# A streaming row sum: four rows per partition in the first load instead of one

## The chip, the cores and the metric

The kernel runs on one core of one Trainium2 chip. The metric is the device time of one execution in microseconds (us); the median of three runs stands for it. GB/s are 10^9 bytes per second, KiB and MiB are powers of two.

## The reference

```python
batch, seq, dim = 32, 512, 1024
x = np.random.randn(batch, seq, dim).astype(np.float32)
multiplier = 0.5

def reference(x, multiplier):
    return (np.sum(x, axis=-1) * multiplier).astype(np.float32)
```

So 16384 rows of 1024 float32 values (67.1 MB) are read, each is summed and multiplied by 0.5, and 64 KiB are written.

## The kernel before

The 16384 rows are spread over 128 partitions, 128 rows each. They are read in three groups, all on one DMA queue, issued by SyncE (SP):

- **The lead**: one row per partition, the last 128 rows of `x`, into a buffer of its own (`lead`). It is the first load (512 KiB, 4 KiB for each partition).
- **Seven blocks** (`b` = 0 to 6) of B = 16 rows per partition, 8 MiB each, 64 KiB for each partition. Partition p owns 112 consecutive rows of `x`, so a partition's piece of a block is contiguous. Blocks rotate through three buffers, `buf[b % 3]`. The load of block b from 3 on waits on SP until DVE (VectorE) has reduced block b - 3 (`freed`, line 122).
- **The tail**: the remaining 15 rows per partition (`tail = B - 1`), 15 consecutive rows of `x` for each partition. It is loaded in three pieces of 7, 5 and 2 rows into the buffer that block 4 has left (`pieces`, line 157), and the fifteenth row comes in two parts of 608 and 416 columns into `end` (line 162). All five loads are issued in a row once block 4 is reduced.

The sums are made as follows.

- The lead is summed on DVE before block 0 (line 128). The sums lie in column 0 of `lead_sq`, 32x32 transposes (line 129) turn them into 4 rows of 32 values, and these are stored as 4 pieces of 128 B.
- A block is one `reduce_sum` on DVE over 16 rows (line 134) and one small multiplication (line 140). In block 6, DVE takes 8 rows and ACT (ScalarE) the other 8, one `activation` with an accumulator for each row (`act_row`, line 90).
- The tail's rows are shared out by hand (`on_act`, line 175): DVE sums a row by adding its two halves with an accumulator (`dve_sum`, line 100), ACT with `act_row`. The end row is summed by DVE in two steps, `first` and `final`, where `final` also adds the result of `first`.

There are three stores, all on SP's queue: `early` for the 112 rows per partition of the blocks (line 167, after block 6), `lead_store` (line 171) right behind it, and `store` for the tail (line 195), after the last sum. SP then waits for all three to land, and the kernel ends.

Before the kernel is built, the loads that wait for nothing (the lead and blocks 0 to 2) are moved into the program's entry block, so that SP issues them ahead of the start barrier (`start_loads_at_entry`).

Of the kernel before, what the change touches and what calls it, by code (L numbers as in the profile page):

```python
# [9 lines left out]
def kernel(  # L10
# [13 lines left out]
    nc = tc.nc  # L24
# [4 lines left out]
    P = nc.NUM_PARTITIONS  # L29
# [3 lines left out]
    x_flat = x.flatten_outer_dims()  # L33
    N, D = x_flat.shape
    rows = N // P
    out_flat = out.rearrange("b s -> (b s)")
    mul = float(multiplier)

    B = 16
    n_blocks = rows // B  # L40
    assert N == P * rows and rows == n_blocks * B
    own = rows - B
    tail = B - 1
    lead0 = P * (own + tail)
    x_rows = x_flat[0 : P * own, :].rearrange("(p c) d -> p c d", p=P)
    x_last = x_flat[P * own : lead0, :].rearrange("(p c) d -> p c d", p=P)
    x_lead = x_flat[lead0:N, :]
    out_rows = out_flat[0 : P * own].rearrange("(p c) -> p c", p=P)
    out_last = out_flat[P * own : lead0].rearrange("(p c) -> p c", p=P)
    out_lead = out_flat[lead0:N].rearrange("(q c) -> q c", c=32)  # L50

    def sbuf(name, *shape):
        return ctx.enter_context(nc.sbuf_tensor(name, list(shape), fp32)).ap()

    bufs = 3
    buf = [sbuf(f"xb{i}", P, B, D) for i in range(bufs)]
    sums = sbuf("sums", P, rows)
    res = sbuf("res", P, rows)
    cut = 608
    at = 640  # L60
    end = sbuf("end", P, at + D - cut)
    S = 32
    lead = sbuf("lead", P, D)
    lead_sq = sbuf("lead_sq", P, S)
    lead_tr = sbuf("lead_tr", P, S)

    def sem(name):
        return nc.alloc_semaphore(name=name)

    dve_done = sem("dve_done")  # L70
    act_done = sem("act_done")
    counts = {"dve": 0, "act": 0}

    def marks(i, engine):

        s = dve_done if engine == "dve" else act_done
        i.then_inc(s, 1)
        counts[engine] += 1
        return counts[engine]

    def load(name, dst, src, free=None):
        landed = sem(name)
        i = nc.sync.dma_start(out=dst, in_=src)  # L83
        if free is not None:
            i.wait_op(dve_done, free, "sem-ge")
        i.then_inc(landed, 16)
        return landed

    def act_row(t, r, col):
        return nc.scalar.activation(  # L90
            out=t[:, r, :],
            in_=t[:, r, :],
            func=mybir.ActivationFunctionType.Copy,
            scale=mul,
            accum_out=res[:, col : col + 1],
        )

    def dve_sum(row, dst, scale):
        mid = row.shape[-1] // 2
        return nc.vector.tensor_tensor_reduce(  # L100
            out=row[:, 0:mid],
            in0=row[:, 0:mid],
            in1=row[:, mid:],
            scale=scale,
            scalar=0.0,
            op0=ADD,
            op1=ADD,
            accum_out=dst,
        )

    marks(nc.vector.memset(end[:, at - 2 : at], 0.0), "dve")  # L111
    zeroed = marks(nc.vector.memset(lead_sq, 0.0), "dve")  # L112
    freed = []
    lead_landed = load("lead_landed", lead, x_lead)
    for b in range(n_blocks - 1):
        c0 = b * B
        t = buf[b % bufs]
        landed = load(
            f"landed{b}",
            t,  # L120
            x_rows[:, c0 : c0 + B, :],
            freed[b - bufs] if b >= bufs else None,
        )
        h = B if b < n_blocks - 2 else B // 2
        if b == 0:
            nc.vector.wait_ge(lead_landed, 16)
            nc.vector.wait_ge(dve_done, zeroed)
            summed = marks(dve_sum(lead, lead_sq[:, 0:1], mul), "dve")
            turned = nc.vector.transpose(out=lead_tr, in_=lead_sq)  # L129
            turned.wait_op(dve_done, summed, "sem-ge")  # L130
            marks(turned, "dve")
        nc.vector.wait_ge(landed, 16)
        done = marks(
            nc.vector.reduce_sum(  # L134
                out=sums[:, c0 : c0 + h], in_=t[:, 0:h, :], axis=mybir.AxisListType.X
            ),
            "dve",
        )
        freed.append(done)
        scaled = nc.vector.tensor_single_scalar(  # L140
            out=res[:, c0 : c0 + h],
            in_=sums[:, c0 : c0 + h],
            scalar=mul,
            op=mybir.AluOpType.mult,
        )
        scaled.wait_op(dve_done, done, "sem-ge")
        early_dve = marks(scaled, "dve")
        if h < B:
            nc.scalar.wait_ge(landed, 16)
            for r in range(h, B):  # L150
                i = act_row(t, r, c0 + r)
            early_act = marks(i, "act")

    c0 = (n_blocks - 1) * B
    t = buf[(n_blocks - 1) % bufs]
    nc.sync.wait_ge(dve_done, freed[n_blocks - 1 - bufs])
    pieces = [(0, 7), (7, 12), (12, 14)]
    landed = [
        load(f"landed_p{k}", t[:, lo:hi, :], x_last[:, lo:hi, :])
        for k, (lo, hi) in enumerate(pieces)  # L160
    ]
# [6 lines left out]
    early.wait_op(act_done, early_act, "sem-ge")  # L168
    early_stored = sem("early_stored")
    early.then_inc(early_stored, 16)  # L170
    lead_store = nc.sync.dma_start(out=out_lead, in_=lead_tr[0:P:S, :])
    lead_stored = sem("lead_stored")
    lead_store.then_inc(lead_stored, 16)

    on_act = {4, 5, 6, 10, 11, 13}
    for k, (lo, hi) in enumerate(pieces):
        on = [r for r in range(lo, hi) if r in on_act]
        nc.scalar.wait_ge(landed[k], 16)
        for r in on:
            i = act_row(t, r, c0 + r)  # L180
        late_act = marks(i, "act") if k == len(pieces) - 1 else None
        on = [r for r in range(lo, hi) if r not in on_act]
        nc.vector.wait_ge(landed[k], 16)
        for r in on:
            dve_sum(t[:, r, :], res[:, c0 + r : c0 + r + 1], mul)
# [1 line left out]
    first = dve_sum(end[:, 0:cut], end[:, at - 1 : at], 1.0)  # L187

    first.then_inc(landed_end[1], 1)
    final = dve_sum(end[:, at - 2 :], res[:, rows - 2 : rows - 1], mul)  # L190
    final.wait_op(landed_end[1], 17, "sem-ge")
    done = marks(final, "dve")

# [71 lines left out]
```

## Time and profile before

| what | value |
|---|---|
| median of 3 runs | 160.72 us (160.58 to 160.73) |
| the profiled execution | 160.62 us |
| its span, first to last instruction | 159.3 us |
| DVE busy | 120.2 us (75%), 39 instructions |
| ACT busy | 16.3 us (10%), 29 instructions |
| DMA packets | 2168, 67.18 MB, mean 422 GB/s |
| time of the packets, share of 16 engines' span | 98.0% |

The profile shows one execution. The span leaves out what lies before the first and behind the last instruction, 1.3 us here. The busy time of an engine counts its instructions of arithmetic only; the DMA share is the mean busy share of the core's 16 DMA engines. The timeline gives the start of every instruction in us from the start of the span, and in brackets how long its engine had been idle and what ended that. A DMA issue has a time to landing, from the issue on SP to the semaphore that tells that all data is there.

### The profile page before, as it was taken

The page shows a single profiled execution, that of the slowest core. Times are in us where ns is not written, and L with a number is a line of the kernel's source. Part 1 is how long each engine was busy: PE and PEld are TensorE (multiplying, and loading weights), DVE is VectorE, ACT ScalarE, POOL GpSimd, SP SyncE. Part 2 cuts the span into 40 slices and gives each one's busy share as a digit, 9 for nine tenths or more (in the row PEclk, how much of TensorE's full clock was granted, in tenths as well). Part 3 has the DMA queues.
Part 4 walks back from the last instruction along what each step waited for, and adds up shares of the span by engine and source line. Part 5 has one row for each costly group of instructions (what it writes and reads, how often), then busy time and mean ns, then how long its engine had stood idle before and what let it go on. Part 6 is the DMA issues. An engine that isn't in the chain of part 4 may idle for free.

```text
span 159.3 us, 128 instructions
## 1 busy us (share of the span) xinstructions
DVE 120.2 (75%) x39; ACT 16.3 (10%) x29; POOL 0.2 (0%) x4
## 2 busy tenths in 40 slices
DVE  2000029999499995999869997899959999599744
ACT  2000000000000000000000000000000000099844
POOL 0000000000000000000000000000000000000000
DMA  9969989899699699699699898996996996999994
GB/s 395 510 280 527 411 379 527 379 411 527 263 527 527 263 527 527 263 527 494 296 527 428 362 527 379 411 527 280 510 527 263 527 527 263 436 403 433 442 397 144
DMA packets 2168, 67.18 MB, mean 422 GB/s; under 512 B 504, under 2 KB 632, under 8 KB 888
## 3 DMA queue, kind: packets, MB, share of 16 engines
q1 hardware_dynamic: 2168, 67.18, 98.0%
HBM read 67.11 MB, written 0.07 MB: 422 GB/s over the span
## 4 chain that ended last, share of the span: by engine, by line
DMA 75%; DVE 22%; SPq 1%; issue 0%
DMA xb<-in_x_dram 52%; DMA end<-in_x_dram 24%; DVE sums L134 22%; SPq L83 1%; DVE end L100 1%; DVE res L140 0%; DVE res L100 0%
## 5 line engine op out<-in xcount | busy, mean ns | idle before, releaser
L134 DVE TENSOR_REDUCE sums<-xb 128x16 f32<-128x16384 f32 (+1 forms) x7 | 112.0, 16001 | 30.3 <-DMA xb<-in_x_dram 30.3
L90 ACT ACTIVATE xb<-xb 128x1024 f32<-128x1024 f32 x14 | 14.6, 1046 | 138.1 <-DMA xb<-in_x_dram 138.0
L100 DVE CUSTOM_DVE_ANT_0 xb<-xb 128x512 f32<-128x512 f32 x8 | 5.1, 689 | 3.9 <-DMA xb<-in_x_dram 3.9
L90 ACT ACTIVATION_READ_ACCUMULATOR xb<-xb 128x1 f32 x14 | 2.6, 188 | 0.0
L111 DVE MEMSET end<- 128x2 f32 x1 | 0.1, 60 | 2.9 <-PEq L26 2.9
L90 ACT ACT_TABLE_LOAD x1 | 1.3, 1283 | 2.9 <-PEq L26 2.9
L140 DVE TENSOR_SCALAR res<-sums 128x16 f32<-128x16 f32 (+1 forms) x7 | 1.2, 174 | 0.2
L100 DVE CUSTOM_DVE_ANT_0 end<-end 128x304 f32<-128x304 f32 (+1 forms) x2 | 0.9, 428 | 0.1
L100 DVE CUSTOM_DVE_ANT_0 lead<-lead 128x512 f32<-128x512 f32 x1 | 0.7, 693 | 0.2 <-DMA lead<-in_x_dram 0.2
L100 DVE DVE_READ_ACCUMULATOR2_ANT res<- 128x1 f32 x9 | 0.8, 83 | 0.0
L129 DVE STREAM_TRANSPOSE lead_tr<-lead_sq 128x32 f32<-128x32 f32 x1 | 0.2, 211 | 0.0
L246 POOL MEMSET const-bfloat16-1.0<- 128x1 bf16 x1 | 0.1, 101 | 0.0
L246 POOL MEMSET const-uint8-127<- 128x1 uint8 x1 | 0.1, 101 | 0.0
L246 POOL MEMSET const-float32-0.0<- 128x1 f32 x1 | 0.1, 98 | 0.2 <-issue 0.2
L246 POOL MEMSET const-float32-1.0<- 128x1 f32 x1 | 0.1, 98 | 0.0
L112 DVE MEMSET lead_sq<- 128x32 f32 x1 | 0.1, 85 | 0.0
L100 DVE DVE_READ_ACCUMULATOR2_ANT end<- 128x1 f32 x1 | 0.1, 84 | 0.0
L100 DVE DVE_READ_ACCUMULATOR2_ANT lead_sq<- 128x1 f32 x1 | 0.1, 83 | 0.0
## 6 DMA issues: line engine op xcount, KB each, us to landing
xb<-in_x_dram SPq DMA_DIRECT2D x1, 3584.0 KB, 29.9
xb<-in_x_dram SPq DMA_DIRECT2D x1, 2560.0 KB, 35.7
xb<-in_x_dram SPq DMA_DIRECT2D x1, 1024.0 KB, 37.7
lead<-in_x_dram SPq DMA_DIRECT2D x1, 512.0 KB, 3.2
end<-in_x_dram SPq DMA_DIRECT2D x1, 304.0 KB, 37.9
end<-in_x_dram SPq DMA_DIRECT2D x1, 208.0 KB, 38.0
xb<-in_x_dram SPq DMA_DIRECT2D x7, 40.8
out_dram<-res SPq DMA_DIRECT2D x1, 56.0 KB, 9.6
```

The source lines that it names most:

```text
L83: i = nc.sync.dma_start(out=dst, in_=src)
L90: return nc.scalar.activation(out=t[:, r, :], in_=t[:, r, :], func=mybir.ActivationFunctionType.Copy, scale=mul, accum_out=res[:, col : co ...
L100: return nc.vector.tensor_tensor_reduce(out=row[:, 0:mid], in0=row[:, 0:mid], in1=row[:, mid:], scale=scale, scalar=0.0, op0=ADD, op1=ADD, ...
L111: marks(nc.vector.memset(end[:, at - 2 : at], 0.0), "dve")
L112: zeroed = marks(nc.vector.memset(lead_sq, 0.0), "dve")
L129: turned = nc.vector.transpose(out=lead_tr, in_=lead_sq)
L134: nc.vector.reduce_sum(out=sums[:, c0 : c0 + h], in_=t[:, 0:h, :], axis=mybir.AxisListType.X),
L140: scaled = nc.vector.tensor_single_scalar(out=res[:, c0 : c0 + h], in_=sums[:, c0 : c0 + h], scalar=mul, op=mybir.AluOpType.mult,)
L246: nc = _bacc.Bacc("TRN2", target_bir_lowering=False, num_devices=1)
```

## The change

The lead gets four rows per partition instead of one (`L = 4`): the last 512 rows of `x`, four consecutive rows for each partition, 16 KiB each, 2 MiB in all. It goes into the buffer of block 2 (`buf[2]`), which is free until block 2 is loaded. ACT sums its four rows instead of DVE, into `lead_res` (128 x 4), with the multiplication in the same instruction. The load of block 2 now waits for ACT's last sum of the lead, so that it is no longer among the loads at the entry. The zeroed square, the transpose and their buffers are gone, and `lead_store` writes 16 B for each partition, 128 pieces, instead of 4 pieces of 128 B.

The tail has 12 rows per partition instead of 15, in pieces of 5, 4 and 2 rows and the end row. Of its rows ACT takes 3, 4, 7, 8 and 10, DVE the others. The end row's split, the blocks and the order of the stores stay.

```diff
-    tail = B - 1
+    L = 4
+    tail = B - L
     lead0 = P * (own + tail)
...
-    x_lead = x_flat[lead0:N, :]
+    x_lead = x_flat[lead0:N, :].rearrange("(p c) d -> p c d", p=P)
...
-    out_lead = out_flat[lead0:N].rearrange("(q c) -> q c", c=32)
+    out_lead = out_flat[lead0:N].rearrange("(p c) -> p c", p=P)
...
-    S = 32
-    lead = sbuf("lead", P, D)
-    lead_sq = sbuf("lead_sq", P, S)
-    lead_tr = sbuf("lead_tr", P, S)
+    lead = buf[2]
+    lead_res = sbuf("lead_res", P, L)
...
-    def load(name, dst, src, free=None):
+    def load(name, dst, src, free=None, on=None):
         landed = sem(name)
         i = nc.sync.dma_start(out=dst, in_=src)
         if free is not None:
-            i.wait_op(dve_done, free, "sem-ge")
+            i.wait_op(dve_done if on is None else on, free, "sem-ge")
...
-    def act_row(t, r, col):
+    def act_row(t, r, dst):
...
-            accum_out=res[:, col : col + 1],
+            accum_out=dst,
...
-    zeroed = marks(nc.vector.memset(lead_sq, 0.0), "dve")
     freed = []
-    lead_landed = load("lead_landed", lead, x_lead)
+    lead_landed = load("lead_landed", lead[:, 0:L, :], x_lead)
...
-            freed[b - bufs] if b >= bufs else None,
+            freed[b - bufs] if b >= bufs else lead_act if b == 2 else None,
+            act_done if b == 2 else None,
         )
         h = B if b < n_blocks - 2 else B // 2
         if b == 0:
-            nc.vector.wait_ge(lead_landed, 16)
-            nc.vector.wait_ge(dve_done, zeroed)
-            summed = marks(dve_sum(lead, lead_sq[:, 0:1], mul), "dve")
-            turned = nc.vector.transpose(out=lead_tr, in_=lead_sq)
-            turned.wait_op(dve_done, summed, "sem-ge")
-            marks(turned, "dve")
+            nc.scalar.wait_ge(lead_landed, 16)
+            for r in range(L):
+                i = act_row(lead, r, lead_res[:, r : r + 1])
+            lead_act = marks(i, "act")
...
-    pieces = [(0, 7), (7, 12), (12, 14)]
+    pieces = [(0, 5), (5, 9), (9, 11)]
...
-    lead_store = nc.sync.dma_start(out=out_lead, in_=lead_tr[0:P:S, :])
+    lead_store = nc.sync.dma_start(out=out_lead, in_=lead_res)
+    lead_store.wait_op(act_done, lead_act, "sem-ge")
...
-    on_act = {4, 5, 6, 10, 11, 13}
+    on_act = {3, 4, 7, 8, 10}
...
-    final = dve_sum(end[:, at - 2 :], res[:, rows - 2 : rows - 1], mul)
+    final = dve_sum(end[:, at - 2 :], res[:, own + tail - 1 : own + tail], mul)
```

More of the change, by code (lines that the diff above doesn't have):

```diff
@@ L150 @@
             for r in range(h, B):
-                i = act_row(t, r, c0 + r)
+                i = act_row(t, r, res[:, c0 + r : c0 + r + 1])
             early_act = marks(i, "act")
@@ L179 @@
         for r in on:
-            i = act_row(t, r, c0 + r)
+            i = act_row(t, r, res[:, c0 + r : c0 + r + 1])
         late_act = marks(i, "act") if k == len(pieces) - 1 else None
```

## The prediction

> **What bounds the kernel now.** I read the page's chain first, then the DMA issues, then the busy time between landings, the timeline of the two ends, and last 0.1 us windows.
>
> ```profile
> ## 4 chain that ended last, share of the span: by engine, by line
> DMA 75%; DVE 22%; SPq 1%; issue 0%
> ```
>
> ```profile
> xb<-in_x_dram SPq DMA_DIRECT2D x7, 40.8
> out_dram<-res SPq DMA_DIRECT2D x1, 56.0 KB, 9.6
> out_dram<-res SPq DMA_DIRECT2D x1, 7.5 KB, 1.4
> ```
>
> The chain's 22% for DVE is the release of a buffer: a block load is issued when a reduction ends. But a block load takes 40.8 us to land and the loads follow each other every 19.36 us, so the new one stands some 21 us behind others. The releases could be later without emptying the queue. The 56 KB store lands 9.6 us after issue, at 157.6: it waits behind the loads, so the queue keeps its order.
>
> The next rows are stretches between landings; the columns are length, DVE, ACT and POOL busy (instructions), clock, DMA share, GB/s.
>
> ```profile
> 42.25:61.61 19.36, 17.39 (x2) 0.00 (x0) 0.00 (x0) 1.00 1.00 433
> 139.02:153.63 14.61, 11.30 (x11) 11.66 (x23) 0.00 (x0) 1.00 0.99 426
> 153.63:156.12 2.49, 1.92 (x6) 2.18 (x4) 0.00 (x0) 1.00 0.98 400
> ```
>
> Between landings the DMA share is 1.00. An 8 MiB block takes 19.36 us, 433 GB/s, so one row of every partition (512 KiB) takes 1.21 us. DVE works 17.39 of each 19.36 us and waits the rest. The kernel is bound by the bytes that it reads, plus its start (first packets at about 1.05 us) and its end (from the landing of the end row's first piece at 156.84 to 159.3).
>
> The timeline rows (start, us, what, idle before) at the end:
>
> ```profile
> 139.02 8.69 DVE L134 TENSOR_REDUCE sums<-xb 128x8 f32<-128x8192 f32 x1 [1.93 <-DMA xb<-in_x_dram]
> 147.82 0.69 DVE L100 CUSTOM_DVE_ANT_0 xb<-xb 128x512 f32<-128x512 f32 x1
> 153.63 0.69 DVE L100 CUSTOM_DVE_ANT_0 xb<-xb 128x512 f32<-128x512 f32 x1 [3.28 <-DMA xb<-in_x_dram]
> 156.12 0.69 DVE L100 CUSTOM_DVE_ANT_0 xb<-xb 128x512 f32<-128x512 f32 x1 [0.57 <-DMA xb<-in_x_dram]
> 156.87 0.48 DVE L100 CUSTOM_DVE_ANT_0 end<-end 128x304 f32<-128x304 f32 x1
> 157.80 0.35 SPq L195 DMA_DIRECT2D out_dram<-res  x1
> ```
>
> DVE sits idle 3.28 us before the second tail piece and 0.57 us before the third: these idles are the cover that the change spends.
>
> **The change, part by part.**
>
> *Bytes moved from the tail to the lead.* Three rows go from the tail to the front: 3 x 1.21 = 3.63 us. Every block landing shifts by that: the lead from 3.2 to 6.9, block 0 from 22.81 to 26.44, block 6 from 139.02 to 142.65. Then the first two pieces hold 9 rows instead of 12, so the second lands at 153.63 + 3.63 - 3.63 = 153.63 as before; the 2-row piece and the end row keep their sizes, 156.12 and 156.84. Sum: 0.
>
> *DVE at the tail.* Block 6's half takes from 139.02 to 147.82, 8.80 us, so it ends at 151.45. The first piece has 3 rows for DVE, 0.61 us from start to start, 1.92 with the last one's accumulator: 153.37. Idle before the second piece falls from 3.28 to 0.26 us. That piece has 2 rows (1.30 us, to 154.93), against 156.12. So DVE could be late by 0.26 + 1.19 = 1.45 us in all before the third piece's row starts later. Cost 0.
>
> *ACT at the tail.* Its 8 rows of block 6 end 8.50 us after landing, 151.15; two rows of the first piece (1.04 + 1.06 + 0.19) end by 153.4, before 153.63. Its later pieces are as before. Cost 0.
>
> *Removed from DVE.* The `lead` sum, the transpose and one memset, about 1.1 us near 3 us, where DVE waits 18.62 us for block 0: nothing gained.
>
> *ACT sums the lead, and block 2's load waits for it.* ACT is idle for 134.9 us there. Four rows take 4.3 us (139.02 to 143.3 in block 6), so the mark comes at about 11.2 us, and the load of block 2 is issued then instead of near 1.3. Queued behind it on SP is block 3's load, which waits for DVE to free block 0 anyway: 26.44 + 17.22 = 43.7. Block 2 is needed by the queue when block 1 has landed, 42.25 + 3.63 = 45.9. Cover: 34 us. At 43.7 block 2 is all still queued. Cost 0; were the cover gone, each us of late issue would be a us of time.
>
> *Packet size of the lead.* The 0.1 us windows:
>
> ```profile
> 1.60:1.70 0.10, 0.00 (x0) 0.00 (x0) 0.00 (x0) 1.00 0.84 328
> 5.10:5.20 0.10, 0.00 (x0) 0.00 (x0) 0.00 (x0) 1.00 12.14 5243
> 152.70:152.80 0.10, 0.00 (x0) 0.00 (x0) 0.00 (x0) 1.00 0.79 328
> 157.10:157.20 0.10, 0.10 (x1) 0.10 (x2) 0.00 (x0) 1.00 0.00 0
> 158.70:158.80 0.10, 0.00 (x0) 0.00 (x0) 0.00 (x0) 1.00 0.56 46
> ```
>
> A window books a packet whole where it starts; share x 1.6 us over the packets is the time of one. 4 KiB (lead): 8 packets, 0.168 us each. 64 KiB (blocks): 8 packets, 2.43 each. 8 KiB (third piece): 4 packets, 0.316 each. By the 64 KiB rate, 4 KiB would be 0.152 and 8 KiB 0.304: the excess is 16 and 12 ns, per packet rather than per byte. Each of these loads is 128 packets, 8 for an engine, before and after: the lead 4 KiB to 16 KiB, the tail pieces 28 to 20 and 20 to 16. The number does not change: 0. Ends: if 16 KiB packets lose nothing, -0.13 us (8 x 16 ns); if the lead's loss of 10% goes with its bytes, 4.84 x 0.10 - 0.13 = +0.35. I take 0, since the 8 KiB row loses half the share that the 4 KiB row does.
>
> *Other addresses.* Tail partitions lie 48 KiB apart instead of 60. The trace has 448 KiB at 433 GB/s, and 60 KiB at 12 rows (6.29 MB) in 14.61 us, 431. Nothing shows 48. Ends: the old tail's loss against 433 is 14.61 - 14.52 = 0.09, so -0.09; if 12 rows lose the 3% that the third piece does (2.49 against 2.42), 14.5 x 0.03 = +0.44. I take 0: 48 stands near 60, and both neighbours are within 0.6%.
>
> *The stores.* The early store moves by 3.63 us, from 148.0 to 151.6, the lead's store to about 152.0; both still wait in the queue until the loads end near 157.0. The lead's store grows from 4 pieces of 128 B to 128 of 16 B, 8 for an engine, ahead of the final store. The nearest row is the final store's own 128 pieces of 60 B: all of them start between 158.6 and 158.9, in 0.3 us, and the shares of those three windows sum to 0.92, 0.09 us of an engine's time. Engines are empty from 157.1 to 158.6, so 0.3 us is hidden five times over. Ends: 0 and the rival below. The final store has 48 B pieces for 60: 0.
>
> Here a rule speaks against the change. The Trainium skill (DMA: Bandwidth & Descriptors, Specifications) says that below 512 B the engine reads, modifies and writes, and its section Latency and other measured facts gives an HBM access 0.2 us. An estimate from that page, with the pieces one after another, is 8 x 0.2 = 1.6 us, 157.1 to 158.7: the sum by it would be +0.1 us. The 60 B pieces lie below that limit too, and the trace has 8 of them on an engine in 0.3 us, so it does not bear out the serial reading.
>
> Sum: 0 on the profiled execution's 160.62 (span 159.3 and 1.3 around it). The median is 160.72, 0.1 above that execution. I forecast **160.7**.
>
> **Rivals.**
>
> *A slower stream* (slower). Lead or tail loads lose rate as above: +0.35 or +0.44, 161.1. For: the tail already runs below 433. Against: per-packet losses explain that. It decides from the first ns, since nothing covers DMA time. 0.12.
>
> *The 16 B pieces hold the final store* (slower). If each waited for its write, at the 0.3 us between the final store's last packet (158.9) and its landing (159.2), 8 would end at 157.1 + 2.4 = 159.5, and the final store's packets start 0.9 late: 161.6. It decides from 1.5 / 8 = 0.19 us a piece. Against: the 60 B pieces. 0.05.
>
> *DVE becomes the bound* (slower). It decides past 1.45 us of lateness; the two stretches it would come from sum to 12.0 us of DVE work, so they would have to run 12% longer; at 20% the time is +1.0, 161.7. Against: the same forms vary by 1% in the trace. 0.01.
>
> *A better start* (faster). Block 0 lands 19.56 us after the lead, and block 1 19.44 after that, against 19.36: 0.28 us that a longer first load may absorb, and 0.09 at the tail: -0.37, 160.35. Against: these gaps are those of landings on engines that drift apart, not of missing bytes. 0.11.
>
> *The new wait is late*, or the queue drains (34 us of cover): 0.01.
>
> **How the numbers follow.** No change within 0.2% (0.32 us, about what a measurement of this kernel tells from none): 0.70. Slower by more: 0.12 + 0.05 + 0.01 + 0.01 = 0.19. Faster by more: 0.11. The range: the low end takes in most of the better start, 160.4; the high end the slower stream, 161.1. Outside remain the store, DVE and the late wait (0.07) and the far parts of two others (about 0.1).
>
> **What would show it.** Right: the lead lands near 6.9, block 6 near 142.65, DVE's idle before the second piece is near 0.26, the last load lands near 156.84, and the final store is issued near 157.80. The slower stream would show as a longer stretch from the lead to block 0, or from block 6 to the second piece (11.0 us). The store rival would show as a final store that takes over 1.4 us to land. I am wrong if any block interval departs from 19.36, or if DVE's idle before the third piece is gone.

## The result, and the profile after

The changed kernel takes 161.45 us (median of 6 runs, 161.25 to 161.90), the kernel before on the same chip 160.59 us (6 runs, 160.56 to 160.73). The ratio is 1.0054, with a 95% interval of 1.0041 to 1.0067: the change costs 0.86 us, more than twice the 0.32 us that a measurement tells apart. The forecast was no change, 160.7, with a range of 160.4 to 161.1.

The profiled execution took 161.38 us, span 160.1, against 160.62 and 159.3: 0.76 us more, and this is what the trace has to explain. The page's chain has the same shape:

```profile
## 4 chain that ended last, share of the span: by engine, by line
DMA 75%; DVE 22%; SPq 1%; issue 0%
```

The stretches between the same landings as before (columns: length, DVE, ACT and POOL busy, clock, DMA share, GB/s), with one row added for the first 3 us:

```profile
1.00:3.00 2.00, 0.06 (x1) 0.61 (x1) 0.00 (x0) 1.00 0.98 254
...
46.43:65.79 19.36, 17.39 (x3) 0.00 (x0) 0.00 (x0) 1.00 1.00 433
143.18:154.19 11.01, 10.69 (x9) 10.51 (x21) 0.00 (x0) 1.00 0.98 413
154.19:156.68 2.49, 1.31 (x4) 2.19 (x5) 0.00 (x0) 1.00 0.98 401
```

The middle and the tail are as worked out: a block in 19.36 us, nine tail rows in 11.01 (9 x 1.21 = 10.89, and 0.12 over that against the 0.09 of before), two rows in 2.49. The first row is the odd one. In the first 2 us of the stream the 16 DMA engines are busy throughout (0.98) and yet move 254 GB/s instead of 433: the same bytes keep an engine busy 1.7 times as long as in the row of a block. The timeline:

```profile
7.76 1.06 ACT L89 ACTIVATE xb<-xb 128x1024 f32<-128x1024 f32 x1 [4.08 <-DMA xb<-in_x_dram]
...
27.09 17.22 DVE L131 TENSOR_REDUCE sums<-xb 128x16 f32<-128x16384 f32 x1 [24.57 <-DMA xb<-in_x_dram]
...
46.43 17.22 DVE L131 TENSOR_REDUCE sums<-xb 128x16 f32<-128x16384 f32 x1 [1.91 <-DMA xb<-in_x_dram]
...
154.19 0.69 DVE L99 CUSTOM_DVE_ANT_0 xb<-xb 128x512 f32<-128x512 f32 x1 [0.28 <-DMA xb<-in_x_dram]
...
156.68 0.69 DVE L99 CUSTOM_DVE_ANT_0 xb<-xb 128x512 f32<-128x512 f32 x1 [1.18 <-DMA xb<-in_x_dram]
157.44 0.47 DVE L99 CUSTOM_DVE_ANT_0 end<-end 128x304 f32<-128x304 f32 x1
...
158.38 0.33 SPq L193 DMA_DIRECT2D out_dram<-res  x1
```

The lead lands at 7.7 us instead of 6.9, block 0 at 27.09 instead of 26.44, block 1 at 46.43 instead of 42.25 + 3.63 = 45.88. I take block 1 as the measure of the start, since from there on the intervals are even: **the start costs 0.55 us**. Nothing is given back later: DVE starts on the end row's first piece at 157.44 instead of 156.87, and the final store is issued 0.58 later.

```profile
out_dram<-lead_res SPq DMA_DIRECT2D x1, 2.0 KB, 5.9
out_dram<-res SPq DMA_DIRECT2D x1, 6.0 KB, 1.6
```

The final store lands 1.6 us after its issue instead of 1.4. From its issue to the end of the execution it is 161.38 - 158.38 = 3.00 us, against 160.62 - 157.80 = 2.82: **the end costs 0.18 us**. 0.58 + 0.18 = 0.76.

### The profile page after: what moved, and what is told of

The parts are those of the page before. It is cut to its first block, busy times and chain, and to the rows that moved or that the text cites. A ratio compares the mean times of both kernels' runs of the same rounds, so it can differ in the third digit from the quotient of the medians.

```text
span 160.1 us, 125 instructions
## 1 busy us (share of the span) xinstructions
DVE 118.0 (74%) x31; ACT 19.4 (12%) x35; POOL 0.2 (0%) x4
## 4 chain that ended last, share of the span: by engine, by line
DMA 75%; DVE 22%; SPq 1%; issue 0%
DMA xb<-in_x_dram 54%; DVE sums L131 22%; DMA end<-in_x_dram 21%; SPq L82 1%; DVE end L99 1%; DVE res L137 0%; DVE res L99 0%
## 5 line engine op out<-in xcount | busy, mean ns | idle before, releaser
L89 ACT ACTIVATE xb<-xb 128x1024 f32<-128x1024 f32 x17 | 17.7, 1046 | 136.0 <-DMA xb<-in_x_dram 136.0
L99 DVE CUSTOM_DVE_ANT_0 xb<-xb 128x512 f32<-128x512 f32 x6 | 3.9, 690 | 1.5 <-DMA xb<-in_x_dram 1.5
L89 ACT ACTIVATION_READ_ACCUMULATOR xb<-xb 128x1 f32 x17 | 3.2, 189 | 0.0
```

Source lines behind the costliest of these rows:

```text
L89: return nc.scalar.activation(out=t[:, r, :], in_=t[:, r, :], func=mybir.ActivationFunctionType.Copy, scale=mul, accum_out=dst,)
L99: return nc.vector.tensor_tensor_reduce(out=row[:, 0:mid], in0=row[:, 0:mid], in1=row[:, mid:], scale=scale, scalar=0.0, op0=ADD, op1=ADD, ...
```

## The experiments

Each kernel is one edit away from the kernel before or the changed kernel. "Start" is the landing of block 1 against 42.25 us (one row in the lead) or 45.88 (four rows); "end" is the time from the final store's issue to the end of the execution, both from the profiled execution. One execution of each run has a trace, so how far such a figure repeats has to be known. Four variants that start just like the kernel before (the two stores of 48 B, the two halves and the 4 B pieces) have block 1 at 42.19 to 42.30, and the changed kernel and four variants with its lead at 46.41 to 46.57. So I read no difference in the start below about 0.15 us.

### The start: packet size, places, region

**Rows apart.** The changed kernel, with the lead in four loads:

```diff
-    lead_landed = load("lead_landed", lead[:, 0:L, :], x_lead)
+    lead_landed = [load(f"lead_landed{r}", lead[:, r, :], x_lead[:, r, :]) for r in range(L)]
```

> The changed kernel, but its lead comes in four loads of one row per partition each: packets of 4 KiB instead of 16 KiB, from the same addresses, into the same buffer. Theory A (the first packets of each engine are slow in proportion to their size: the 21 or so 16 KiB packets that start before 2.2 us take some 1.0 us instead of 0.61): 4 KiB packets start like those of the kernel before, block 0 lands near 26.5 us instead of 27.09, and the time falls to 160.8. Theory B (the addresses: engines that read at places 64 KiB apart at the same time hinder one another): the first packets lie at the same places, so block 0 still lands near 27.1 and the time stays at 161.4. Both: 24 more packets on each engine at some 14 ns would add 0.3 us.

162.13 us, ratio 1.0100 (1.0086 to 1.0113); block 1 at 47.29, start +1.41, end 3.14. Smaller packets from the same places start worse, not better: block 1 is 0.86 us later than in the changed kernel, of which 0.3 was expected for 24 more packets on each engine. Theory A falls; B expected no gain, but not the rest of this loss either.

**Block first.** The kernel before, with the lead issued behind block 0:

```diff
-    lead_landed = load("lead_landed", lead, x_lead)        # ahead of the loop
+            lead_landed = load("lead_landed", lead, x_lead)  # b == 0, behind load("landed0", ...)
```

> The kernel before, but block 0 is loaded first and the lead second: the first packets are of 64 KiB, at places 1792 KiB apart from engine to engine. Without a loss at the start block 0 lands at 22.81 - 1.21 = 21.6 us. Theory A (packets that start cold are slow in proportion to their size): it lands at 22.1 or later, and the time rises by 0.5 us or more, to 161.1 at least. Theory B (places 64 KiB apart): no collision, 21.6 us, and the time stays at 160.6.

160.80 us, 1.0016 (1.0007 to 1.0025); block 1 at 42.40, start +0.15, end 2.80. The packets that start cold are 16 times as large as the lead's and cost 0.15 us. A again predicts too much.

**Another pitch, 448 KiB.** The changed kernel, with the lead from the place of block 0's rows:

```diff
+    lead_landed = load("lead_landed", lead[:, 0:L, :], x_rows[:, 0:L, :])
```

> The changed kernel, but the lead reads the first four rows of each partition's block 0 (16 KiB packets at a pitch of 448 KiB instead of 16 KiB), so that its sums are those of other rows. Theory A (size of the first packets): block 0 still lands near 27.1 us, the time stays at 161.4. Theory B (places): the first packets take 0.6 us, block 0 lands near 26.4 and the time falls to 160.8.

161.39 us, 1.0051 (1.0037 to 1.0064); block 1 at 46.16, start +0.28, end 3.30. Half of the start's loss is gone with no other change than the places. The total does not show it, because the end, at 3.30 us, is the longest of all kernels that store the lead in 16 B pieces.

**Thin lead.** The kernel before, with gaps between its 4 KiB packets:

```diff
-    x_lead = x_flat[lead0:N, :]
+    x_lead = x_flat[N - 4 * P : N, :].rearrange("(p c) d -> p c d", p=P)[:, 0, :]
```

> The kernel before, but its lead reads one row of every four of the last 512 rows: the same 4 KiB packets, now at a pitch of 16 KiB instead of 4, so that its 128 sums are partly those of other rows. Theory B' (the places of the first reads: with four partitions to an engine, engines stand 64 KiB apart instead of 16 and hinder one another until they drift apart): block 1 lands 0.5 us or more after the 42.25 us of before, and the time rises to 161.1 or more. Theory A (size of the first packets) and theory D (a cold start of the chip that costs the same whatever is read first): 4 KiB packets as before, block 1 at 42.25, 160.6.

161.63 us, 1.0066 (1.0052 to 1.0079); block 1 at 43.27, start +1.02, end 2.79. Its first 2 us and block 1:

```profile
1.00:3.00 2.00, 0.00 (x0) 0.05 (x1) 0.00 (x0) 1.00 0.90 211
...
43.27 17.22 DVE L134 TENSOR_REDUCE sums<-xb 128x16 f32<-128x16384 f32 x1 [1.94 <-DMA xb<-in_x_dram]
```

This is the cleanest pair of the study: same packets, same bytes, same queue, and only the places of 128 reads cost 1.0 us. A cold start at a fixed price (D) falls too.

**Pitch of 20 KiB.** The changed kernel, with a gap of one row behind each partition's four:

```diff
-    x_lead = x_flat[lead0:N, :].rearrange("(p c) d -> p c d", p=P)
+    x_lead = x_flat[N - 5 * P : N, :].rearrange("(p c) d -> p c d", p=P)[:, 0:L, :]
```

> The changed kernel, but the lead reads the first four rows of every five of the last 640 rows: 16 KiB packets at a pitch of 20 KiB instead of 16, engines 80 KiB apart, so that its sums are partly those of other rows. Theory B' (places equal up to a multiple of 64 KiB): the start is as good as before's, block 1 lands at 42.25 + 3.63 = 45.9 instead of 46.43, and the time falls by 0.5 to 160.9. Theory A (packet size): no change, 46.4 and 161.4.

162.08 us, 1.0089 (1.0075 to 1.0103); block 1 at 46.95, start +1.07, end 3.14. The rule of B' (places equal up to a multiple of 64 KiB) expected a gain of 0.5 us and got a loss of 0.5. The places matter, but not by that rule.

**Another region.** The changed kernel, with the same form of lead from the first 512 rows of `x`:

```diff
+    x_lead = x_flat[0 : P * L, :].rearrange("(p c) d -> p c d", p=P)
```

> The changed kernel, but the lead reads the first 512 rows of x instead of the last 512, in the same form (16 KiB packets at a pitch of 16 KiB), so that its sums are those of other rows. Theory F (how the first reads lie to one another sets the loss at the start): block 1 lands at 46.4 as in the changed kernel, the time is 161.4. Theory G (the region at the end of x is slow to start on): it lands near 45.9, and the time falls to 160.9.

161.64 us, 1.0069 (1.0055 to 1.0083); block 1 at 46.41, start +0.53, end 2.89. The start's loss is that of the changed kernel, so it belongs to the form of the lead and not to its region. That the two agree to 0.02 us is luck: the profiled execution, at 161.23, is the fastest of six that reach up to 162.08, and the slower ones have no trace.

**Lead second.** The changed kernel with block 0 issued first:

```diff
-    lead_landed = load("lead_landed", lead[:, 0:L, :], x_lead)        # ahead of the loop
+            lead_landed = load("lead_landed", lead[:, 0:L, :], x_lead)  # b == 0, behind load("landed0", ...)
```

> The changed kernel, but block 0 is loaded first and the lead second. Theory F1 (the pattern of the lead costs only while all engines start at once): the start is that of the kernel with block 0 first, 0.15 us after the kernel before, so block 1 lands at 45.88 + 0.15 = 46.0 and the time is 161.0. Theory F2 (the pattern is slow wherever it stands in the queue): the 0.55 us stay, block 1 lands at 46.4 or later, and the time at 161.4.

161.29 us, 1.0037 (1.0025 to 1.0049); block 0 lands at 21.96, the lead at 26.83, block 1 at 46.19; start +0.31, end 3.02. The two landings, as DVE and ACT start on them:

```profile
21.96 17.22 DVE L131 TENSOR_REDUCE sums<-xb 128x16 f32<-128x16384 f32 x1 [19.45 <-DMA xb<-in_x_dram]
...
26.83 1.06 ACT L89 ACTIVATE xb<-xb 128x1024 f32<-128x1024 f32 x1 [23.17 <-DMA xb<-in_x_dram]
```

Between them are 4.87 us, against 4 x 1.21 = 4.84 at full rate, and from the lead to block 1 19.36: **the same 2 MiB that lose time as the first load lose nothing as the second**, which is the mechanism of F1. By the numbers F1 is missed: it expected block 1 at 46.0 and 161.0 us. The 0.31 us stand ahead of block 0's landing, in its own cold start, 0.16 more than in the block-first run.

**Row first.** The changed kernel, with the old lead (128 rows without gaps, 4 KiB each) ahead of three rows per partition:

```diff
+    x_one = x_flat[N - P : N, :]
+    x_three = x_flat[lead0 : N - P, :].rearrange("(p c) d -> p c d", p=P)
...
+    one_landed = load("one_landed", lead[:, 0, :], x_one)
+    lead_landed = load("lead_landed", lead[:, 1:L, :], x_three)
```

> The changed kernel, but the lead comes in two loads: first one row per partition from the last 128 rows, 4 KiB packets without gaps, as in the kernel before, then three rows per partition, 12 KiB each, without gaps (the sums come out in another order of rows). If the pattern of the very first load alone sets the loss at the start, block 1 lands at 45.9 as worked out from the kernel before, and the time falls by 0.5 to 160.9. If the 2 MiB of the lead are slow whatever stands ahead of them, it stays at 46.4 and 161.4.

161.09 us, 1.0033 (1.0022 to 1.0044); block 1 at 46.21, start +0.33, end 2.91. Between the two expectations: the first load alone does not set the loss, but the old first load removes 0.2 of the 0.55 us.

**Dense rows.** As the rows apart, but each of the four loads reads 128 rows without gaps:

```diff
-    x_lead = x_flat[lead0:N, :].rearrange("(p c) d -> p c d", p=P)
+    x_lead = x_flat[lead0:N, :].rearrange("(c p) d -> p c d", p=P)
...
```

> The changed kernel with the lead in four loads of 4 KiB packets, as in the run with the rows apart, but each load reads 128 rows without gaps (as the lead of the kernel before does) instead of every fourth row; the sums come out in another order of rows. Theory F (how the first reads lie to one another sets the start's loss): block 1 lands at 45.9, with 24 more packets on an engine at 14 ns at most at 46.2, against 47.29 with the rows apart, and the time falls below 161.5 from 162.1. If the number of small loads makes the loss, it lands at 47.3 again and the time is 162.1.

161.94 us, 1.0076 (1.0051 to 1.0100); block 1 at 47.17, start +1.29, end 3.00. By the total and by block 1 (47.3 expected) it agrees with "the number of small loads". The windows at the start of the two kernels say more; dense rows first, rows apart second:

```profile
1.00:3.00 2.00, 0.00 (x0) 0.00 (x0) 0.00 (x0) 1.00 0.98 317
3.00:6.00 3.00, 0.06 (x1) 2.15 (x2) 0.00 (x0) 1.00 0.89 345
```

```profile
1.00:3.00 2.00, 0.00 (x0) 0.00 (x0) 0.00 (x0) 1.00 0.86 213
3.00:6.00 3.00, 0.06 (x1) 1.83 (x2) 0.00 (x0) 1.00 1.01 363
```

In the first 2 us the dense rows do better, 317 against 213 GB/s, but behind them the engines run partly empty (share 0.89), and the gain is lost. So four small loads at the head have a price of their own, which I did not take apart.

**One store.** The changed kernel, with tail and lead in one region of 16 rows for each partition (the lead's 16 KiB packets at a pitch of 64 KiB), the lead's sums in the last four result columns, and one final store of 64 B pieces:

```diff
+    x_end = x_flat[P * own : N, :].rearrange("(p c) d -> p c d", p=P)
+    x_last = x_end[:, 0:tail, :]
+    x_lead = x_end[:, tail:B, :]
...
+    lead_res = res[:, own + tail : rows]
...
-    lead_store = nc.sync.dma_start(out=out_lead, in_=lead_res)
...
-    store = nc.sync.dma_start(out=out_last, in_=res[:, own : own + tail])
+    store = nc.sync.dma_start(out=out_last, in_=res[:, own:rows])
```

> The changed kernel, but tail and lead share the last 2048 rows with 16 consecutive rows for each partition (12 of the tail, 4 of the lead, both at a pitch of 64 KiB), ACT's sums of the lead go into the last four result columns, and the final store writes all 16 columns, 64 B for each partition; there is no store of the lead. Theory E (the final store takes longer to land with 48 B pieces than with 60 B because of how the pieces lie): 64 B pieces land in 1.4 us or less instead of 1.6, and the time falls by 0.2 to 0.5. If the length of the landing is chance, it stays at 1.6 to 1.9. The start: theory B' gives no improvement (engines 256 KiB apart), block 1 at 46.4; so does A.

160.71 us, 1.0002 (0.9994 to 1.0011); block 1 at 45.95, start +0.07, end 2.77. Its first 2 us and its stores:

```profile
1.00:3.00 2.00, 0.06 (x1) 0.61 (x1) 0.00 (x0) 1.00 1.07 360
```

```profile
out_dram<-res SPq DMA_DIRECT2D x1, 56.0 KB, 6.0
out_dram<-res SPq DMA_DIRECT2D x1, 8.0 KB, 1.4
```

Both losses are gone, and a lead of four rows takes the time of a lead of one. The wait of block 2's load for ACT is still there, so it is not what makes the changed kernel's start slow. The expectation for the start (no improvement) was wrong, by the same wrong rule as above.

**One store, one row.** The kernel before with the same region and one final store:

```diff
+    x_lead = x_end[:, tail, :]
...
-            summed = marks(dve_sum(lead, lead_sq[:, 0:1], mul), "dve")
...
+            marks(dve_sum(lead, res[:, rows - 1 : rows], mul), "dve")
...
+    store = nc.sync.dma_start(out=out_last, in_=res[:, own:rows])
```

> The kernel before, but the tail's 15 rows and the lead's one row share the last 2048 rows with 16 consecutive rows for each partition, DVE puts the lead's sum straight into the last result column, and the final store writes 16 columns, 64 B for each partition; the transpose and the lead's store are gone. The lead's 4 KiB packets lie 64 KiB apart. If the loss at the start goes with the pitch as the 16 KiB packets at 64 KiB had it (0.07 us), block 1 lands at 42.3, the final store in 1.4 us or less, and the time is 160.4 to 160.7. If 4 KiB packets with gaps between them start slowly at any pitch, as they did at 16 KiB (1.0 us), it is 161.5.

161.04 us, 1.0030 (1.0018 to 1.0041); block 1 at 42.70, start +0.45, end 2.78. This lies between the two expectations: at the same pitch of 64 KiB, 4 KiB packets lose 0.45 us where 16 KiB packets lost 0.07.

The starts with a single lead or block in front:

| first load | bytes in a row @ pitch | start, us |
|---|---|---|
| kernel before | 4 KiB @ 4 KiB | 0 |
| one store | 16 @ 64 | +0.07 |
| block first; lead second | 64 @ 448 | +0.15; +0.31 |
| another pitch | 16 @ 448 | +0.28 |
| one store, one row | 4 @ 64 | +0.45 |
| changed kernel; four more with its lead | 16 @ 16 | +0.55; +0.53 to +0.69 |
| thin lead | 4 @ 16 | +1.02 |
| pitch of 20 KiB | 16 @ 20 | +1.07 |

How the first reads lie in memory changes the start by up to 1.0 us with nothing else changed. Which property of the places decides is open: neither the size of the packets, nor the pitch, nor having no gaps orders this table. The steps of 0.15 us and less in it are within what repeats.

### The end: where the 0.2 us behind the last issue come from

**Store early.** The changed kernel, with the lead's store issued behind block 2's load near 12 us:

```diff
+        if b == 2:
+            lead_store = nc.sync.dma_start(out=out_lead, in_=lead_res)
...
```

> The changed kernel, but the lead's store is issued right behind block 2's load, near 12 us, so that its 16 B pieces land in the middle of the blocks and not ahead of the final store. Theory C (the 0.2 us by which the final store takes longer to land, 1.6 against 1.4 us, come from the 16 B pieces): it lands in 1.4 us, and the time falls by 0.2 to 161.2. Rival (the final store's own pieces of 48 B instead of 60 B, or chance): it still takes 1.6 us and the time stays at 161.4. If small writes hold up the loads around them, a block interval grows from 19.35 by a few tenths.

162.63 us, 1.0126 (1.0113 to 1.0140), the end 3.11. The landings of blocks 1, 2 and 3:

```profile
46.57:67.54 20.97, 17.39 (x3) 0.00 (x0) 0.00 (x0) 1.00 1.03 431
67.54:86.26 18.72, 17.39 (x3) 0.00 (x0) 0.00 (x0) 1.00 0.96 413
```

Two blocks take 39.69 us instead of 38.71. 2 KiB in 128 pieces, put between two 8 MiB loads, delay the stream by 1.0 us, where a few tenths were thought possible: DVE's spare time between landings is no cover for that, since the stream is the bound. And the end stays long, so C falls: the pieces need not stand just ahead of the final store.

**48 B at a pitch of 60 B**, and **48 B without gaps**: the kernel before, with 12 of 15 columns sent.

```diff
+    store = nc.sync.dma_start(out=out_last[:, 0:12], in_=res[:, own : own + 12])   # pitch of 60 B
...
+    out_last = out_flat[P * own : P * (own + 12)].rearrange("(p c) -> p c", p=P)   # no gaps
+    store = nc.sync.dma_start(out=out_last, in_=res[:, own : own + 12])
```

> The kernel before, but the final store sends 12 of its 15 columns, 48 B for each partition at a pitch of 60 B, so that three columns of the output are not written. Theory E, if it is the size of the pieces: the final store lands in 1.6 us or more instead of 1.4, and the time rises by 0.2 to 160.8. If it is the pitch of 48 B or chance, 1.4 and 160.6.

> The kernel before, but the final store sends 12 of its 15 columns to pieces of 48 B that follow each other without a gap, as in the changed kernel, so that part of the output is not written or is written to other places. Theory E' (the final store's extra 0.2 to 0.5 us come from the pitch of 48 B, since 48 B at a pitch of 60 B landed in 1.4 us): it lands in 1.6 to 1.9 us, and the time is 160.8 to 161.1. If the extra comes from something else in the changed kernel: 1.4 us and 160.6.

160.56 us, 1.0000 (0.9992 to 1.0009), and 160.61 us, 0.9998 (0.9989 to 1.0006); both land in 1.4 us, ends 2.80 and 2.79. The final store's own pieces are not the cause: E and E' fall.

**Two halves.** The kernel before, with block 4 in two loads of 8 rows:

```diff
+        if b == 4:
+            half = load("half", t[:, 0:8, :], x_rows[:, c0 : c0 + 8, :], freed[1])
...
```

> The kernel before, but block 4 is loaded in two halves of 8 rows: one more load on the queue, no small pieces. From the issue of the final store to the end of the execution there are 2.8 us in the kernel before and its variants, and 2.9 to 3.3 in the changed kernel and those of its variants that store the lead in 16 B pieces, even where these landed 90 us earlier. Theory P (the place of the final store in the queue: the store of 128 pieces, or any further load over all engines, moves it): 3.0 to 3.1 us and 160.9. Theory Q (the 16 B pieces themselves): 2.8 us and 160.6.

160.85 us, 1.0019 (1.0009 to 1.0028): the total is the one that P gave. Its profiled execution has an end of 3.45 us, but at 161.42 it is also 0.57 above this kernel's median. Block 4's interval is 19.56 us and the final store's issue 0.17 later, which with an end of 2.8 makes 160.77, near the median. So the halves may have cost their 0.2 us in the stream, and of the end this run says little; it does not refute P.

**4 B pieces.** The kernel before, with the lead's sums stored straight from the column:

```diff
-    lead_store = nc.sync.dma_start(out=out_lead, in_=lead_tr[0:P:S, :])
+    lead_store = nc.sync.dma_start(out=out_lead, in_=lead_sq[:, 0:1])
```

(`out_lead` is then cut into 128 pieces of one value.)

> The kernel before, but its lead is stored as 128 pieces of 4 B straight from the 128 sums instead of 4 pieces of 128 B from the transposed square. Theory Q (small pieces): from the final store's issue to the end 3.0 us or more instead of 2.8, and the time is 160.9. Theory P (place in the queue) gives the same, so that this run counts together with the one of the two halves. If neither, 2.8 us and 160.6.

164.83 us, 1.0278 (1.0251 to 1.0305): a loss of 4.2 us, where 0.3 was expected. The stores, and SP's wait for the lead's:

```profile
out_dram<-res SPq DMA_DIRECT2D x1, 56.0 KB, 16.6
out_dram<-lead_sq SPq DMA_DIRECT2D x1, 0.5 KB, 16.4
out_dram<-res SPq DMA_DIRECT2D x1, 7.5 KB, 7.1
```

```profile
SPq L200 <- DMA out_dram<-lead_sq: 6.6, 1, 6.6
```

The store issued at 148.37 lands at 164.8, 7.7 us after the last load packets at about 157.1, and the early store and the final one with it. This execution, at 166.25 us, is the slowest of six and 1.4 above their median. Its windows at the end:

```profile
157.00:157.25 0.25, 0.25 (x1) 0.24 (x2) 0.00 (x0) 1.00 0.08 9
...
158.50:158.75 0.25, 0.00 (x0) 0.00 (x0) 0.00 (x0) 1.00 0.32 27
...
159.00:159.25 0.25, 0.00 (x0) 0.00 (x0) 0.00 (x0) 1.00 0.00 0
```

The final store's packets start from 158.6 on, 0.8 us after its issue, as in the kernel before, and from 159.0 to the end no packet starts. So the 4 B pieces do not keep the engines busy and do not hold the final store's packets: what comes 6 to 7 us late is the landing of all three stores. The transpose that the change removed, 0.2 us of DVE far off the path, saved this. With 16 B pieces the removal is nearly harmless. Whether the size of the pieces decides, or that all 128 fall into 512 adjacent bytes, this run does not separate.

**No lead store.** The changed kernel without it:

```diff
-    lead_store = nc.sync.dma_start(out=out_lead, in_=lead_res)
```

> The changed kernel without the lead's store, so that the last 512 sums are not written. Theories P and Q: from the final store's issue to the end 2.8 us instead of 3.0 to 3.1, and the time falls by 0.2 to 0.3, to 161.2; the start keeps its 0.55 us (block 1 at 46.4). If the end is slow for another reason in the changed kernel, 3.0 and 161.4.

161.30 us, 1.0040 (1.0028 to 1.0052); block 1 at 46.56, start +0.68, end 2.78, the final store lands in 1.4 us. The end is short again, and the start keeps its loss, so that the lead's store is shown as the cause of the longer end.

**End row whole.** The changed kernel with the end row in one load, one transfer less:

```diff
+    landed_end = load("landed_e", end[:, 0:D], x_last[:, tail - 1, :])
...
+    final = dve_sum(end[:, 0:D], res[:, own + tail - 1 : own + tail], mul)
```

> The changed kernel, but the end row comes in one load and DVE sums it in one step, so that there is one transfer less over all engines ahead of the final store (15 with it, as in the kernel before, instead of 16), while the lead is still stored in 16 B pieces. Theory P (the final store's place among the transfers): from its issue to the end of the execution 2.8 us instead of 3.0. Theory Q (the 16 B pieces ahead of it): 3.0 or more. The end row's load lands as late as the second part did and its sum takes 0.8 us, so the issue itself comes some 0.2 us later and the whole time hardly moves (161.3 by P, 161.6 by Q).

161.46 us, 1.0051 (1.0038 to 1.0065); the final store issued at 158.69, 0.31 later, end 2.97. One transfer less does not shorten the end: P falls in this form, though the total lies between the two expectations.

Together: the eight profiled executions of kernels that store no 16 B or 4 B pieces, the two halves left aside, have ends of 2.77 to 2.82 us, the ten that store 16 B pieces 2.89 to 3.30. So the 0.2 us belong to the lead's store. Whether it is the 16 B or the 128 pieces of one more store is not separated: no run stores the lead in 128 larger pieces. The place of the 0.2 us can be read from the changed kernel's windows:

```profile
159.20:159.30 0.10, 0.00 (x0) 0.00 (x0) 0.00 (x0) 1.00 0.54 38
159.30:159.40 0.10, 0.00 (x0) 0.00 (x0) 0.00 (x0) 1.00 0.37 24
```

The final store's packets start 0.8 to 1.0 us after its issue at 158.38, no later than in the kernel before (issue at 157.80, packets between 158.6 and 158.9). They are not held. The landing behind the last of them takes longer: some 0.6 us, from 159.4 to 160.0, where the kernel before took 0.3, from 158.9 to 159.2. Why it is late, and why it stays so when the lead's store is 90 us earlier, I can't explain.

## Why the prediction was wrong, by its own steps

- **Bytes moved, DVE and ACT at the tail, the new wait: right.** DVE's idle before the second piece was forecast 0.26 and measured 0.28, before the third 1.19 and 1.18; nine rows took 11.01 us; ACT's four sums took 4.3 us, and block 2's load had its 34 us of cover. The sum of 0 for the moved bytes is what the one-store kernel measures: 160.71 against 160.62.
- **"Packet size of the lead": the step that failed.** It priced the lead by the time of a packet in single 0.1 us windows (16 and 12 ns more per packet), found the number of packets unchanged, and took 0 from a range of -0.13 to +0.35. Measured: +0.55. The loss is not a price per packet: the thin lead has the same 128 packets of 4 KiB as the kernel before and loses 1.02 us. In its place the runs show a loss of the first load alone (as the second load the same 2 MiB take 4.87 us, the full rate), set by how its reads lie, while the engines are busy and slow together. The trace of before held a sign of it:

```profile
1.00:2.40 1.40, 0.00 (x0) 0.00 (x0) 0.00 (x0) 1.00 0.95 328
```

Over this whole stretch a packet of the lead takes 0.95 x 1.6 us x 14 / 112 packets = 0.19 us, 25% over the 0.152 of the 64 KiB rate, and not the 0.168 of the one window that I took, and I read the excess as a price of 4 KiB packets. With 0.19 the upper end would have been, by my estimate, 4.84 x 0.25 - 8 x 0.038 = +0.9 instead of +0.35.
- **"Other addresses": right for the tail, not asked for the lead.** 48 KiB of pitch cost about 0.03 us in the tail (11.01 against 10.98). But the lead's pitch changed as well, from 4 to 16 KiB, and that step has only the tail: here a term was left at nothing without a reason, and it is the one that the thin lead measures.
- **"The stores": wrong by a little.** Cost 0 because hidden; measured 0.15 to 0.2. The step asked when the final store's packets can start, and there it was right; it did not ask whether they land as soon as before. The rival (pieces that wait one after another, and packets of the final store that start 0.9 late) is not what happened, in the 4 B run either: there the packets start on time and the landing is late. So the rival's sign, a final store that takes over 1.4 us to land, did come, but not from the rival's mechanism. The Trainium skill (DMA: Bandwidth & Descriptors, Specifications) says that below 512 B the engine reads, modifies and writes. No run here shows that read; 48, 60 and 64 B pieces, far below that limit, all land in 1.4 us as the final store, and only the 16 B and 4 B pieces come with a price.
- **The rivals.** "A slower stream" is what happened, with 0.12 of the chance and a price of 161.1; its place was named (lead or tail), its size was short because it came from the same few windows. The range ended at that price and so missed 161.45. "A better start" had a longer first load gain up to 0.28 us; the first load lost 0.55.

## What to carry to other kernels

When the stream of loads is the bound, the first load's form is on the path even if its data are wanted late: give it a stretch of its own in the sum, and price it from the whole of that stretch and not from the steady rate. Where its places change, the trace of before does not have the price; here it was found only by running the variant. In these runs a few bytes in small pieces were cheap only behind the last load and only if the pieces were not tiny: the same 2 KiB cost 1.0 us in mid-stream and 0.2 at the end, and 512 B in 4 B pieces cost 4.2 us. No version beat the kernel before; the one that keeps four rows and loses nothing puts the lead's sums into the final store.

## What the runs showed of the hardware that I had not expected

- The first 2 us of the load stream run at 211 (thin lead) to 360 GB/s (one store) where the lead is the first load, with the engines busy for 0.86 of the time or more; the steady rate is 433. With equal bytes, one first load of 512 KiB costs 0, 0.45 or 1.02 us, and one of 2 MiB 0.07 to 1.07, by where its reads lie.
- A store of 128 adjacent pieces of 4 B landed 7.7 us after the last load packets, in an execution 1.4 us above its run's median, and the stores ahead of it and behind it landed within 0.2 us of it, though no packet started in the last 5.9 us. 128 pieces of 48 to 64 B land in 1.4 us from issue.
- A store of 2 KiB in 16 B pieces between two loads of 8 MiB held the stream by 1.0 us.
